# A hybrid decoder layer on Trainium2: the first 512 columns of x for the residual loaded behind the third branch block instead of behind the fourth

## The chip, the cores and the metric

The kernel runs on one core of one Trainium2 chip. The metric is the device time of one execution in microseconds (us). The core's engines are PE (TensorE, matrix products; PEld is its loading of weights), DVE (VectorE), ACT (ScalarE), POOL (GpSimd) and SP (SyncE, which issues most of the DMA transfers). Each engine works through its own instructions in order; they wait for each other and for DMA transfers through semaphores.

## What is computed

One layer of a decoder trunk over 256 tokens of width 2048, all in float32:

```
mod = silu(c) @ w_ada + b_ada;  shift1, scale1, gate1, shift2, scale2, gate2 = split(mod)
h = rms_norm(x, norm1_gain) * (1 + scale1) + shift1
proj = h @ w_in            # queries, keys, values of three branches, and 3 x 2048 columns of gates
y = sigmoid(g0) * (o_sb @ w_br_sb) + sigmoid(g1) * (o_dil @ w_br_dil) + sigmoid(g2) * (o_gla @ w_br_gla)
x = x + gate1 * (y @ w_out)
h = rms_norm(x, norm2_gain) * (1 + scale2) + shift2
x = x + gate2 * ((silu(h @ w_gate) * (h @ w_up)) @ w_ffn_out)
```

Here o_sb, o_dil and o_gla are the outputs of stick-breaking, dilated and gated linear attention. The change concerns the line `x = x + gate1 * (y @ w_out)`: where and when its x is loaded.

## The kernel before

**Products.** Every float32 product is made of three products of split operands: a value is the sum of a rounded high part and a remainder (`mm3`, L172 to L175). Weights come through `load_weights` (L140 to L170): SP loads 512 KB, two rows of 128 by 512 columns, into one of four `raw` buffers (L151), ACT casts it to `whi` (L165), DVE subtracts to `wlo` (L166). There are four buffers of each kind, so a load waits for the split of the load four before, and a cast waits for the matmuls that read the buffer four before. Such a double row is called a pair below: 12 matmuls of 512 columns in a block that works on both halves of the tokens (t = 0 and 1, 128 tokens each). `block` (L177) runs over k, 16 rows of 128 in y @ w_out, so eight pairs.

**Order of the work.** The program is traced by a framework that then orders the instructions of each engine itself: by priority among those that are ready. Priority is the place in the program; a stretch inside `prio()` is pulled forward by 4000 places. The loads, casts and splits of weights are pulled forward, and so are the residual (L1445) and the background loads of w_ada (L526, L527). The loads of x at L1439 are not.

**Named homes.** `S(tag, ...)` (L98) gives a buffer with a fixed home: a new tile under the same tag can be written once all readers of the old one have ended. Homes A2, A3, A4 and A8, 128 x 1024 float32 each, matter here. `gtags` (L1190) says which gates live there: A2, A3, A4 hold the three gates of the fourth block of 512 columns (and earlier those of the first); A8 holds the second branch's gate of the second block.

**Branch blocks.** `y_block(n)` (L1307) makes 512 columns of y: for each branch a product with its weights, then the gate times the product (L1318, L1320), then the sum (L1321). Gates of the first three blocks are made ahead; those of the fourth by `gate_block(3, br)` after the third branch block (L1343 to L1345). The last reader of A8's gate is therefore in y_block(1), those of the gates in A2, A3, A4 are in y_block(3).

**Output projection and residual.** After the branch blocks L1437 to L1440 load x in four parts of 512 columns, in the order of their use, into A2, A3, A4, A8 (`X2_TAGS`, L1404). Then L1441 to L1448 run three blocks of y @ w_out, 512 columns each, and a fourth follows at L1454 to L1467 with its tokens' halves one after the other. Each block accumulates in two PSUM buffers of a pool of four (`acc`, one for each t). `residual(n, t, ps)` (L1358) does, for each half of the tokens: a product of gate1 and the accumulator into a scratch tile (L1362, its only reader of the accumulator), an addition to x in place (L1363), and a sum of squares on ACT (L1365). The scratch tiles `scr` are three in turn. After both halves `put_away` (L1410) writes the new x to DRAM through the POOL queue; all four parts stay in their homes until the second norm has read them (L1374). Background work runs beside the blocks at given rates: loads of w_ada and their products on DVE (L431), with rates 0.85, 0.55 and 0.1 loads for each pair in the three blocks (`RATES_OP`, L35). Column sums of finished parts are turned on PE by four transposes at a time (L481).

Of the kernel before, what the change touches and what calls it, by code (L numbers as in the profile page):

```python
# [17 lines left out]
P = 128  # L18
T = 256
NT = T // P  # L20
# [3 lines left out]
NB = 512  # L24
# [56 lines left out]
def trunk(ctx: ExitStack, tc: tile.TileContext, I, out):  # L81
    nc = tc.nc
# [11 lines left out]
    def nm(base):  # L94
        uid[0] += 1
        return f"{base}_{uid[0]}"

    def S(tag, shape, dtype=F32):  # L98
        return slot.tile(shape, dtype, tag=tag, name=nm(tag))
# [13 lines left out]
    @contextmanager  # L113
    def prio(offset=AHEAD):

        with tc.high_priority(offset=offset):
            start = tc.cur_priority
            yield
            n = tc.cur_priority - start
        tc.cur_priority += n  # L120
# [56 lines left out]
    def block(pss, act, src, k0, k1, c0, base=0, w=None, tiles=range(NT), go_on=False, more=False, seeded=False,  # L177
              steps=None, pace=None):

        if w is None:
            w = load_weights(src, k0, k1, c0)
        if pace is None:
            pace = 1.0 if tiles[-1] == NT - 1 else 0.0
        for k in range(k0, k1):
            if (k - k0) % 2 == 0:
                tick(state["rate"] * pace)
            if k - k0 == DEFER and later:  # L190
                with tc.issue_after(state["mm"].ins), prio():
                    later.pop()()
            if steps and k - k0 in steps:
                with tc.issue_after(state["mm"].ins), prio():
                    steps[k - k0]()
            wh, wl = w[k - k0]
            for t in tiles:
                h, l = act(base + k, t)
                mm3(pss[t], h, l, wh, wl, k == k0 and not go_on, k == k1 - 1 and not more, seeded)
# [1052 lines left out]
    for j in range(2):  # L1252
# [3 lines left out]
        for t in range(NT):  # L1256
            for h in (2 * j, 2 * j + 1):
                o, c = og[t][:, h, :], t * N_GLA + h
# [5 lines left out]
    for j in range(2):  # L1264
        hi = S(gtag[0][j], [P, 4, T], F32R)
        lo = S(gtag[1][j], [P, 4, T], F32R)
        for t in range(NT):
            o = og[t].rearrange("p h d -> p (h d)")
            ps = misc_bank([P, 4, P])
            for i in range(4):  # L1270
                c = 4 * j + i
# [27 lines left out]
    def transpose_split(src, hi, lo, t, bank=misc_bank):  # L1299

        ps = bank([P, 4, P])
        for i in range(4):
            nc.tensor.transpose(ps[:, i, :], src[:, i * P : (i + 1) * P], ident)  # L1303
        c = slice(t * P, (t + 1) * P)
        split_from_psum(hi[:, :, c], lo[:, :, c], ps)

    def y_block(n, banks=(acc_bank, misc_bank, acc_bank)):  # L1307
        y = S("T3", [P, NT, NB])
        for br, (src, kc, act) in enumerate(
            ((I["w_br_sb"], 6, sb_at), (I["w_br_dil"], 2, dil_at), (I["w_br_gla"], 8, gla_at))  # L1310
        ):
            pss = [banks[br]([P, NB]) for _ in range(NT)]
            block(pss, act, src, 0, kc, n * NB)
            with prio():
                for t in range(NT):
                    g = gates[n, br][:, t, :]
                    if br == 0:
                        nc.vector.tensor_mul(y[:, t, :], g, pss[t])  # L1318
                    else:
                        nc.vector.tensor_mul(g, g, pss[t])  # L1320
                        nc.vector.tensor_add(y[:, t, :], y[:, t, :], g)  # L1321
        hi = S(ytags[n][0], [P, 4, T], F32R)
        lo = S(ytags[n][1], [P, 4, T], F32R)
        def turn():
            for t in range(NT):
                transpose_split(y[:, t, :], hi, lo, t)

        later.append(turn)
        yT.append((hi, lo))
# [9 lines left out]
    y_block(0, (misc_bank, acc_bank, acc_bank))  # L1339
    y_block(1)  # L1340
    y_block(2)
    state["rate"] = RATE_LAST
    for br in range(3):  # L1343
        gate_block(3, br)
# [8 lines left out]
    while "gate1" not in state:  # L1353
        tick(1)
    gate1 = state["gate1"]
    x2 = []
    x2ss = const.tile([P, NT, 4], F32, name="x2ss")
    def residual(n, t, ps):  # L1358

# [41 lines left out]
            nc.vector.tensor_tensor(h2[1][j][:, :, c], hf, hi.bitcast(F32), op=ALU.subtract)  # L1401

    h2_raw = {}
    X2_TAGS = ("A2", "A3", "A4", "A8")  # L1404
    x2_away = []

    def put_away(n):
# [10 lines left out]
    def gate2_bg():  # L1418

        acc = biased([S(tag, [P, 2 * NB]) for tag in ("OS0", "T3")], SEG_GATE2)  # L1420
        yield from ada_segment_steps(acc, SEG_GATE2, None, False, range(GATE2_CUT))
        yield from last_macs()
        for j in range(2):
            nc.gpsimd.dma_start(gate2_away[j], acc[j])
# [9 lines left out]

    ring["tags"] = ("A12", "KD", "KC", "H7")
    bg.append(gate2_bg())
    for n in range(4):  # L1437
        xr = S(X2_TAGS[n], [P, NT, NB])
        nc.sync.dma_start(xr, I["x"][:, n * NB : (n + 1) * NB].rearrange("(t p) c -> p t c", p=P))  # L1439
        x2.append(xr)  # L1440
    for n in range(3):  # L1441
        state["rate"] = RATES_OP[n]
        pss = [acc_bank() for _ in range(NT)]
# [192 lines left out]
    n, pss = 3, o[1]  # L1636
# [42 lines left out]
```

## Time and profile before

| what | value |
|---|---|
| three runs | 1582.02 us median (1581.56, 1582.02, 1584.25) |
| the profiled execution, its own time | 1581.39 us |
| its span, first to last instruction | 1579.6 us |
| mean granted clock of TensorE over the span | 0.999 |
| HBM read and written | 395.68 MB and 5.24 MB |
| DMA packets of the SP and ACT queues | 75.4% of 16 engines' span |

The times in the profile count from the start of the span. In a row of the timeline stand start, length, engine, line, operation, what is written and read, the count, and in brackets the idle time of that engine just before and what ended it. Buffer names are shown without their numbers, so A2 and A8 are both A. SPq is SP's queue of instructions: its rows are the issues of transfers. Rows of the view by stretches give the busy time of each engine in the stretch, the granted clock of TensorE (1.00 is full) and the share and rate of the DMA engines. In the list of waits stand who waited, for what, the total, the count and the longest. The ends of matmuls are modelled and overlap, so their pace is read from start to start.

### The profile page before, as it was taken

What the parts mean: (1) busy time and instruction counts of PE and PEld (TensorE: products, weight loads), DVE (VectorE), ACT (ScalarE), POOL (GpSimd) and SP (SyncE); (2) the same over time, 40 slices, a digit from 0 to 9 for tenths busy, and PEclk for the clock granted to TensorE, in tenths of its full rate; (3) what the DMA queues carried; (4) which work ended last, traced back from release to release, by engine and by line L of the source; (5) the groups of instructions that cost most, each with busy time, mean ns of one, the idle gap of its engine ahead of it and who ended that gap; (6) DMA issues with size and microseconds to landing.
All of it is one profiled execution on the core that took longest, in us unless ns stands there. A gap on an engine that the chain in (4) does not pass through costs nothing.

```text
span 1579.6 us, 20268 instructions
## 1 busy us (share of the span) xinstructions
PE 1564.1 (99%) x7177; PEld 1292.0 (82%) x7177; DVE 1407.4 (89%) x1728; ACT 879.7 (56%) x1222; POOL 12.6 (1%) x24
## 2 busy tenths in 40 slices
PE   8999999999999999999999999999999999999998
PEld 7878888888888888888877888888888888888887
DVE  6889996888899999987868889999999998989896
ACT  5654448875775554444435645566555555455553
POOL 1000000000000000000000000000000000000000
PEclk9999999999999999999999999999999999999999
DMA  9999987677797778988987897665656566876664
GB/s 336 360 326 323 335 302 240 222 224 223 242 310 255 235 246 267 304 300 309 334 301 252 286 320 228 198 200 200 198 192 222 174 200 236 283 228 201 225 209 138
DMA packets 196317, 402.26 MB, mean 255 GB/s; under 512 B 13102, under 2 KB 28116, under 8 KB 196216
## 3 DMA queue, kind: packets, MB, share of 16 engines
q1 hardware_dynamic: 194952, 397.75, 75.4%
q0 software_dynamic: 1088, 3.16, 0.5%
q8 instruction: 56, 0.92, 0.2%
q14 instruction: 45, 0.37, 0.1%
q10 hardware_dynamic: 176, 0.07, 0.0%
HBM read 395.68 MB, written 5.24 MB: 254 GB/s over the span
## 4 chain that ended last, share of the span: by engine, by line
PE 85%; DVE 6%; ACT 3%; DMA 3%; issue 2%; POOL 0%; SPq 0%; ACTq 0%; DVEq 0%; POOLq 0%
PE acc L175 20%; PE acc L174 20%; PE acc L173 20%; PE misc L173 7%; PE misc L175 7%; PE misc L174 7%; DVE wlo L229 1%; ACT whi L165 1%; DVE wlo L166 1%; DVE OD L229 1%; PE acc L586 1%; PE misc L955 1%; DVE KD L229 1%; DMA raw<-w_in 1%; PE misc L1303 0%
## 5 line engine op out<-in xcount | busy, mean ns | idle before, releaser
L165 ACT CAST whi<-raw 128x1024 fp32r<-128x1024 f32 (+1 forms) x277 | 279.1, 1012 | 287.4 <-PE acc L175 163.6
L166 DVE TENSOR_TENSOR wlo<-raw,whi 128x1024 fp32r<-128x1024 f32 (+1 forms) x277 | 321.9, 1172 | 88.5 <-ACT whi L165 86.9
L173 PE MATMUL acc<-whi,H 128*128 128x512 f32 x1006 | 394.2, 393 | 0.9 <-ACT H L598 0.8
L175 PE MATMUL acc<-whi,H 128*128 128x512 f32 x1006 | 392.7, 391 | 0.5 <-DVE H L605 0.4
L174 PE MATMUL acc<-wlo,H 128*128 128x512 f32 x1006 | 392.4, 390 | 0.8 <-DVE wlo L166 0.7
L175 PEld LDWEIGHTS acc<-whi,H 128*128 128x128 f32 x1006 | 188.7, 188 | 41.1 <-DVE H L605 1.6
L173 PEld LDWEIGHTS acc<-whi,H 128*128 128x128 f32 x1006 | 188.9, 188 | 39.6 <-ACT H L598 1.3
L174 PEld LDWEIGHTS acc<-wlo,H 128*128 128x128 f32 x1006 | 189.0, 188 | 39.3 <-DVE wlo L166 1.7
L243 ACT CAST whi<-raw 128x1024 fp32r<-128x1024 f32 (+1 forms) x130 | 125.5, 982 | 65.5 <-PE acc L175 28.0
L229 DVE TENSOR_TENSOR wlo<-raw,whi 128x1024 fp32r<-128x1024 f32 (+1 forms) x130 | 144.8, 1134 | 13.9 <-ACT whi L243 12.9
L173 PE MATMUL acc<-whi,A 128*128 128x512 f32 x211 | 83.2, 394 | 2.7 <-DVE scr L1362 2.7
L175 PE MATMUL acc<-whi,A 128*128 128x512 f32 x218 | 85.4, 392 | 0.0
L174 PE MATMUL acc<-wlo,A 128*128 128x512 f32 x211 | 82.7, 392 | 0.8 <-DVE wlo L166 0.8
L173 PE MATMUL misc<-whi,H 128*128 128x512 f32 (+1 forms) x209 | 81.0, 388 | 0.0
L175 PE MATMUL misc<-whi,H 128*128 128x512 f32 (+1 forms) x209 | 80.9, 387 | 0.0
L174 PE MATMUL misc<-wlo,H 128*128 128x512 f32 (+1 forms) x209 | 80.9, 387 | 0.0
L431 DVE SCALAR_TENSOR_TENSOR ada<-AR,csil,ada 128x1024 f32<-128x1024 f32 x38 | 48.2, 1280 | 6.0 <-DMA AR<-w_ada 6.0
L173 PEld LDWEIGHTS acc<-whi,A 128*128 128x128 f32 x211 | 39.9, 189 | 11.2 <-DVE scr L1362 3.1
L175 PEld LDWEIGHTS acc<-whi,A 128*128 128x128 f32 x218 | 41.2, 189 | 8.6
L243 ACT CAST whi<-OD 128x1024 fp32r<-128x1024 f32 (+1 forms) x25 | 25.5, 1020 | 40.7 <-DVE OD L229 21.8
L229 DVE TENSOR_TENSOR A<-raw,A 128x512 f32<-128x512 f32 (+2 forms) x53 | 47.2, 898 | 0.7 <-ACT A L243 0.2
L174 PEld LDWEIGHTS acc<-wlo,A 128*128 128x128 f32 x211 | 39.9, 189 | 9.3 <-DVE wlo L166 1.2
(714 smaller groups left out, 3035.6 us busy)
## 6 DMA issues: line engine op xcount, KB each, us to landing
raw<-w_in SPq DMA_DIRECT2D x189, 512.0 KB, 4.9
raw<-w_ffn_in SPq DMA_DIRECT2D x135, 512.0 KB, 4.6
raw<-w_ffn_out SPq DMA_DIRECT2D x73, 512.0 KB, 4.9
AR<-w_ada SPq DMA_DIRECT2D x59, 512.0 KB, 4.8
raw<-w_out SPq DMA_DIRECT2D x32, 512.0 KB, 6.6
OS<-w_ada SPq DMA_DIRECT2D x24, 512.0 KB, 6.9
AR<-w_ffn_in SPq DMA_DIRECT2D x22, 512.0 KB, 4.7
KC<-w_ada SPq DMA_DIRECT2D x21, 512.0 KB, 5.2
```

The costliest lines, as they stand in the source:

```text
L165: state["cast"] = nc.scalar.copy(hi[:, :n, :], raw[:, :n, :])
L166: state["split"] = nc.vector.tensor_tensor(lo[:, :n, :], raw[:, :n, :], hi[:, :n, :].bitcast(F32), op=ALU.subtract)
L173: nc.tensor.matmul(ps, lh, rh, start=start, stop=False, skip_group_check=seeded)
L174: nc.tensor.matmul(ps, lh, rl, start=False, stop=False, skip_group_check=seeded)
L175: state["mm"] = nc.tensor.matmul(ps, ll, rh, start=False, stop=stop, skip_group_check=seeded)
L229: done = nc.vector.tensor_tensor(dst, x, y, op=ALU.subtract)
L243: nc.scalar.copy(hi[:, :n, :], src)
L431: nc.vector.scalar_tensor_tensor(acc, raw, c, acc, op0=ALU.mult, op1=ALU.add)
L586: state["warm"] = nc.tensor.matmul(ps, ones_r, wide, start=True, stop=True)
L955: nc.tensor.matmul(ps[:n, t * N_GLA + h, :].rearrange("p (s l) -> p s l", l=L), at(f, h, t)[:, :n], odd(at(f, h, t)), start=True, stop=True,)
```

## The change

The load of the first 512 columns of x is moved in the program from behind y_block(3) to behind y_block(2), and the homes are dealt anew: the first columns go to A8, the second, third and fourth to A2, A3 and A4. The other three loads stay where they were. Nothing else is changed; no instruction is added or left out.

```diff
     y_block(2)
+    X2_TAGS = ("A8", "A2", "A3", "A4")
+    x2 = []
+
+    def load_x2(n):
+
+        xr = S(X2_TAGS[n], [P, NT, NB])
+        nc.sync.dma_start(xr, I["x"][:, n * NB : (n + 1) * NB].rearrange("(t p) c -> p t c", p=P))
+        x2.append(xr)
+
+    load_x2(0)
     state["rate"] = RATE_LAST
     for br in range(3):
         gate_block(3, br)
...
     gate1 = state["gate1"]
-    x2 = []
...
     h2_raw = {}
-    X2_TAGS = ("A2", "A3", "A4", "A8")
     x2_away = []
...
     bg.append(gate2_bg())
-    for n in range(4):
-        xr = S(X2_TAGS[n], [P, NT, NB])
-        nc.sync.dma_start(xr, I["x"][:, n * NB : (n + 1) * NB].rearrange("(t p) c -> p t c", p=P))
-        x2.append(xr)
+    for n in range(1, 4):
+        load_x2(n)
     for n in range(3):
         state["rate"] = RATES_OP[n]
```

## Prediction

> **What bounds the kernel now.** I read the page's shares first, then the waits of the stretch of the output projection (797 to 870 us), then the chain of waits there, then the instructions in order of time on SP, DVE and PE. The share line of the page:
>
> ```profile
> PE 1564.1 (99%) x7177; PEld 1292.0 (82%) x7177; DVE 1407.4 (89%) x1728; ACT 879.7 (56%) x1222; POOL 12.6 (1%) x24
> ```
>
> PE (TensorE) is busy for 1564.1 of the span's 1579.6 us. So nothing but PE time counts: a change gains what PE waits, or runs slowly, because of the thing changed, and no more. The load of x for the residual shows up in that way. The waits of the stretch 797 to 870 us (total, times, longest):
>
> ```profile
> DVE A L1363 <- DMA A<-x: 4.4, 1, 4.4
> ...
> PE acc L173 <- DVE scr L1362: 2.7, 1, 2.7
> ```
>
> One DVE addition waits for x, and PE waits once for a DVE product. The chain that ended last ties the two together (start, length, what):
>
> ```profile
> 820.73 6.67 DMA A<-x
> 827.42 0.69 DVE A L1363
> 828.11 0.61 DVE scr L1362
> ```
>
> The load of x issued at 820.73 lands 6.67 us later; the addition L1363 (first half of the tokens, columns 0 to 511) takes 0.69; behind it on the in-order DVE queue stands L1362 of the second half, which reads the accumulator that PE wants back. SP's queue says why the load is late, and what an empty A8 is worth:
>
> ```profile
> 654.97 0.37 SPq L1439 DMA_DIRECT2D A<-x  x1
> ...
> 820.31 0.37 SPq L151 DMA_DIRECT2D raw<-w_out  x1
> 820.73 0.46 SPq L1439 DMA_DIRECT2D A<-x  x1
> 823.03 0.37 SPq L151 DMA_DIRECT2D raw<-w_out  x1
> 823.45 0.98 SPq L1439 DMA_DIRECT2D A<-x  x2
> ```
>
> Four loads come from L1439. One is out at 655, three at 820 to 824. The names leave the number of A out, but the homes tell them apart: A2, A3 and A4 hold gates of the fourth block, and their last readers run after 760 us; A8 holds a gate of the second block. DVE's rows for the last reader of A8 (L1321) and of A2 (L1318):
>
> ```profile
> 653.66 1.29 DVE L1321 TENSOR_TENSOR T<-T,A 128x512 f32<-128x512 f32 x2
> ...
> 760.56 1.31 DVE L1318 TENSOR_TENSOR T<-A,acc 128x512 f32<-128x512 f32 x2
> ```
>
> So the load at 654.97, right as A8's last reader ends at 654.95, is that of the **last** 512 columns, which nobody needs before the fourth product block; the first 512 columns, needed first, wait behind weights until 820.73, though A2 is free from 761.87 (760.56 + 1.31).
>
> **What the wait costs PE.** PE in order of time, a normal passage first and then the wait:
>
> ```profile
> 802.49 0.39 PE L175 MATMUL acc<-whi,A 128*128 128x512 f32 x1
> 802.72 0.60 PE L481 MATMUL misc<-ident,ada 128*128 128x128 f32 x4
> 803.07 0.48 PE L173 MATMUL acc<-whi,A 128*128 128x512 f32 x1
> ```
>
> ```profile
> 825.71 0.39 PE L175 MATMUL acc<-whi,A 128*128 128x512 f32 x1
> 828.76 0.80 PE L173 MATMUL acc<-whi,A 128*128 128x512 f32 x1 [2.67 <-DVE scr L1362]
> 829.36 0.63 PE L174 MATMUL acc<-wlo,A 128*128 128x512 f32 x1
> 829.78 0.63 PE L175 MATMUL acc<-whi,A 128*128 128x512 f32 x1
> ...
> 831.49 0.87 PE L481 MATMUL misc<-ident,ada 128*128 128x128 f32 x4
> 832.12 0.48 PE L173 MATMUL acc<-whi,A 128*128 128x512 f32 x1
> ```
>
> Count from start to start. Normal: a matmul starts 0.23 us after the one before (802.49 to 802.72), and four transposes take 0.35 (802.72 to 803.07). From 825.71, undisturbed, PE would come to 825.94, after six matmuls to 827.32 and after the transposes to 827.67. It comes there at 832.12. The wait costs **832.12 - 827.67 = 4.45 us**, of which 2.82 are the late start (828.76 - 825.94) and 1.63 the slow six matmuls and transposes behind it. Those are slow because of the clock (stretch; busy time of PE, PEld, DVE, ACT, POOL; granted PE clock; DMA share; GB/s):
>
> ```profile
> 797.00:820.50 23.50, 23.50 (x111) 19.40 (x111) 17.03 (x17) 8.41 (x8) 0.00 (x0) 1.00 0.89 304
> 820.50:826.10 5.60, 5.59 (x25) 4.31 (x23) 1.23 (x1) 1.05 (x1) 0.00 (x0) 1.00 0.99 349
> 826.10:828.80 2.70, 0.04 (x1) 0.04 (x1) 1.35 (x3) 0.66 (x2) 0.00 (x0) 0.97 1.04 391
> 828.80:832.00 3.20, 3.20 (x9) 2.51 (x10) 1.93 (x3) 1.01 (x4) 0.57 (x1) 0.50 0.64 256
> ```
>
> The granted clock is 0.50 for the 3.20 us after the idle time. The Trainium skill (page TensorE: Matmul & The Clock Gate, Part 1) has the clock fall to half after an idle window of about 3.4 us; taken literally, 2.67 us would be too short, the sum would be 2.82 and the time 1579.2. The trace disagrees: the half clock stands right behind these 2.67 us, the measurement decides, and I give that case no chance of its own.
>
> **The change part by part.** *The load.* Its count stays four: one early, into A8, three late, into A2, A3, A4. x[0] takes the early place. A8 is free at the same moment and the new code stands earlier in program order, so I put the load at 655 us, 140 us before its reader. The SP queue at 655 gets the same 0.37 us entry as before. Gain: 4.45 us.
>
> *What moves with it.* The first residual can now follow its matmuls:
>
> ```profile
> 797.07 0.68 DVE L1362 TENSOR_TENSOR scr<-T,acc 128x512 f32<-128x512 f32 x1
> 797.67 2.36 DVE L166 TENSOR_TENSOR wlo<-raw,whi 128x1024 fp32r<-128x1024 f32 x2
> 801.39 1.23 DVE L166 TENSOR_TENSOR wlo<-raw,whi 128x1024 fp32r<-128x1024 f32 x1 [1.37 <-ACT whi L165]
> ```
>
> L1363, L1362, L1363, three instructions or 0.69 + 0.68 + 0.69 = 2.06 us, move from 827 to about 798. Cover: the splits at 797.67 are the third and fourth pair of the second w_out block, which begins near 797.6; the third is wanted two pairs of 12 x 0.23 us later, at 803.1, and would be done at 798.9 + 2.06 = 801.0; 2.1 us are to spare. DVE also idles 1.37 us before 801.39. Cost 0; without the cover at most 2.06. Two squares on ACT move as well; ACT is busy for 8.41 of 23.50 us there.
>
> *The write-back* of x[0] (L1410, POOL queue) moves from 829.73 to about 800, into the stretch with the DMA share 0.89 at 304 GB/s: 524288 bytes / 304 GB/s = 1.72 us of transfer. The Trainium skill (DMA: Bandwidth & Descriptors, Issuing engines are not separate DMA queues) speaks against the change here: transfers of all queues share the same 16 engines and interleave, so the POOL queue is no way around. Cover: the casts wait longest for PE to give buffers back, so weights stand ahead of PE:
>
> ```profile
> ACT whi L165 <- PE acc L175: 15.8, 11, 3.7
> ```
>
> That is 15.8 us over 11 casts in 797 to 870. Cost 0; without cover 1.72.
>
> *What is late next.* Columns 512 to 1023 now go to A2 and take the old place, 820.73, landing at 827.42. PE doesn't need their accumulators: the third block uses the first block's, free since 798. But DVE's queue holds the split of the third block's fifth pair. The third block starts 24 matmuls before the gap, at 825.94 - 24 x 0.23 = 820.42; pair five is due at 820.42 + 48 x 0.23 + 0.35 = 831.8. Should DVE stand at L1363 until 827.42, then L1363, L1362, L1363 and a split (2.06 + 1.23) end at 830.7; through ACT (square 0.63 + 0.19, cast 1.05, from the rows of those lines, split 1.23, after the first 0.69) at 831.2 (827.42 + 0.69 + 0.63 + 0.19 + 1.05 + 1.23):
>
> ```profile
> 828.14 0.63 ACT L1365 ACTIVATE scr<-A 128x512 f32<-128x512 f32 x1 [6.39 <-DVE A L1363]
> 828.68 0.19 ACT L1365 ACTIVATION_READ_ACCUMULATOR scr<-A 128x1 f32 x1
> ```
>
> In time by 0.6 us: cost 0. Where splits stand ahead of the addition there is no issue at all.
>
> *The next PE wait* follows in the fourth block:
>
> ```profile
> 851.25 0.39 PE L173 MATMUL acc<-whi,A 128*128 128x512 f32 x1
> 852.46 0.50 PE L174 MATMUL acc<-wlo,A 128*128 128x512 f32 x1 [0.81 <-DVE wlo L166]
> ```
>
> 1.21 - 0.23 = 0.98 us. Its loads queue behind the held-up ACT and DVE of 822 to 828; without the hold-up they start earlier and it may vanish (-0.98), or DVE and ACT catch up in another order and it doubles (+0.98, my guess at a bound). I take 0.
>
> Sum: **-4.45 us**, ends -5.43 and -4.45 + 2.06 + 1.72 + 0.98 = +0.31. The profiled execution took 1581.39 us, its span 1579.6; the median of the three runs is 1582.02, 0.63 above. 1582.02 - 4.45 gives **1577.6 us**; the profiled execution should show a span near 1575.2. About 0.2% (3.16 us) is what a measurement of this kernel can tell from no change.
>
> **The rivals.**
>
> 1. *The wait passes to the second 512 columns, in part.* x[1] is issued one place later, at 823.45 as the second of the late loads was, and lands 6.69 later at 830.14. That is 2.4 us after the 827.7 at which L1363 in front of pair five just suffices. PE idles about 2.4: 1577.6 + 2.4 = 1580.0, or 1581.6 with the half clock behind it. For: a DMA share of 0.99 at 820 to 826. Against: the rows of SP show x served between weights at just that point. 15%.
>
> 2. *Slower: x[1] starves.* In the run before, SP came to x only as PE was running out of work; with PE going on, weight loads keep coming, and they go first. Place: DVE at L1363 of the second columns, in front of pair five's split. Price: 1 us of PE per us of landing past 827.7, and 1.63 of half clock. It decides from 830.5 (2.8 + 1.63 eat the 4.45). If x[1] goes out one pair's time (12 x 0.23 = 2.76) behind the last x load of before (823.94, the second of the two issues that fill 0.98 us from 823.45), at 826.7, it lands at 833.4: 5.7 + 1.63 - 4.45 = +2.9, **1584.9**. For: A2 lay free for 59 us (761.87 to 820.73) with nothing issued into it. Against: the third block asks for fewer background loads (rate 0.1 against 0.85 and 0.55), so SP should come to x sooner. 12%.
>
> 3. *The gain is given back later.* PE arrives 4.45 earlier at stages where DVE is 89% busy over the span; if one such stage keeps its old time but for 2 us, 1580. Against: DVE loses its own 4.4 us wait too. 8%.
>
> 4. *The load isn't early*: the order of SP keeps it near 820 in spite of A8. 1582.0. Against: A8 took an x at 654.97. 3%.
>
> **How the numbers follow.** Forecast 62% (own range 1576.1 to 1578.8: the ends of the next PE wait, and the 0.5 by which the fastest run shown lies under the median). Rival 1 15%, rival 2 12%, rival 3 8%, rival 4 3%. Faster by over 0.2%, below 1578.9: the forecast and a third of rivals 1 and 3 with smaller delays, less a little: 0.67. Slower, above 1585.2: rival 2 and the tails of 1: 0.13. Same: the rest, 0.20. The range must reach over rivals 1, 3 and 4 and leaves out rival 2 and some tails: 1575.4 to 1583.0, the low end being 1577.6 - 0.98 less again about 1.2 for later PE waits, an estimate.
>
> **What would show it.** An x load near 655 read near 798; the first additions and squares gone from 827 to 830; no PE wait on L1362; granted clock 1.00 from 797 to 850; L1410's first issue near 800; the same 0.23 us pace throughout the third block. It would be wrong if DVE waits for x at another addition in front of splits that PE needs, if the granted clock drops at another place, or if the wait at 851 grows by more than 1 us.

## The result and the profile after

Twenty runs of each kernel:

| | before | changed |
|---|---|---|
| median | 1581.82 us | 1578.80 us |
| range | 1577.80 to 1586.98 | 1577.94 to 1582.06 |
| profiled execution, its time | 1581.39 us | 1578.55 us |
| its span | 1579.6 us | 1576.7 us |

The ratio is 0.9983 (95% interval 0.9976 to 0.9990). The change gains 3.0 us; 4.45 was forecast. The forecast started from a median of 1582.02 for the kernel before, 0.2 above the 1581.82 here.

In the changed kernel the same code stands in other lines: L1362 is L1371 (product), L1363 is L1372 (addition), L1365 is L1374 (square), L1410 is L1418 (write-back), L1439 is L1348 (load of x). Its share line:

```profile
PE 1562.4 (99%) x7177; PEld 1291.2 (82%) x7177; DVE 1407.6 (89%) x1728; ACT 881.1 (56%) x1222; POOL 12.7 (1%) x24
```

The issues of x on SP's queue (start, length):

```profile
654.66 0.37 SPq L1348 DMA_DIRECT2D A<-x  x1
...
822.00 0.46 SPq L1348 DMA_DIRECT2D A<-x  x1
823.72 0.37 SPq L151 DMA_DIRECT2D raw<-w_out  x1
824.13 0.56 SPq L1348 DMA_DIRECT2D A<-x  x1
826.43 0.37 SPq L151 DMA_DIRECT2D raw<-w_out  x1
826.85 0.46 SPq L1348 DMA_DIRECT2D A<-x  x1
```

Again one load goes out at 655 and three from 820 on, in the homes that the change deals. The first is now that of the first columns; the second columns start at 822.00. PE at the place where it had waited 2.67 us runs on at 0.23 us from start to start:

```profile
825.73 0.39 PE L173 MATMUL acc<-whi,A 128*128 128x512 f32 x1
825.96 0.39 PE L174 MATMUL acc<-wlo,A 128*128 128x512 f32 x1
826.18 0.39 PE L175 MATMUL acc<-whi,A 128*128 128x512 f32 x1
```

The stretches (busy time of PE, PEld, DVE, ACT, POOL; granted clock; DMA share; GB/s) show the full clock where 0.50 had stood, and the DMA share still above 1 there (a packet counts whole in the stretch in which it starts):

```profile
820.50:826.10 5.60, 5.60 (x28) 4.66 (x27) 4.44 (x5) 2.10 (x2) 0.00 (x0) 1.00 0.88 271
826.10:828.80 2.70, 2.70 (x14) 2.23 (x13) 0.30 (x1) 0.00 (x0) 0.00 (x0) 1.00 1.06 406
828.80:832.00 3.20, 3.20 (x16) 2.65 (x15) 2.15 (x6) 1.75 (x4) 0.08 (x1) 1.00 1.06 380
```

DVE still waits for x, now for the second columns; PE does not follow it:

```profile
825.18 1.23 DVE L166 TENSOR_TENSOR wlo<-raw,whi 128x1024 fp32r<-128x1024 f32 x1
829.52 0.69 DVE L1372 TENSOR_TENSOR A<-A,scr 128x512 f32<-128x512 f32 x1 [3.12 <-DMA A<-x]
```

**Where the 2.9 us of span come from.** Three starts of PE in each kernel delimit the third block and the first half of the tokens of the fourth (48 matmuls; at 0.227 us each 10.9 us if PE never waits). Before, then changed:

```profile
820.49 0.39 PE L173 MATMUL acc<-whi,A 128*128 128x512 f32 x1
...
847.17 0.39 PE L173 MATMUL acc<-whi,A 128*128 128x512 f32 x1
...
859.16 0.39 PE L173 MATMUL acc<-whi,A 128*128 128x512 f32 x1
```

```profile
821.18 0.39 PE L173 MATMUL acc<-whi,A 128*128 128x512 f32 x1
...
843.41 0.39 PE L173 MATMUL acc<-whi,A 128*128 128x512 f32 x1
...
855.64 0.39 PE L173 MATMUL acc<-whi,A 128*128 128x512 f32 x1
```

The third block took 26.68 us (847.17 - 820.49) and takes 22.23: **-4.45**, the forecast to the hundredth. The half block behind it took 11.99 and takes 12.23: +0.24. PE's one wait there was 0.81 us at 852.46, on the same split of a weight, and is now

```profile
848.89 0.50 PE L174 MATMUL acc<-wlo,A 128*128 128x512 f32 x1 [1.02 <-DVE wlo L166]
```

The third block begins 0.69 later, and what follows 859 loses 0.6 more (the end moved by -2.9, 859.16 by -3.52). Neither hangs on the change as far as the profiles show. PE works in the same order in both kernels up to 819 and from 835 on, and 0.66 of the 0.69 are there at 731 us already; the 0.6 come in at 1190 us, with a wait of 0.74 that e1 and e8 below, which have the same order of instructions, don't have. An example of such a wait: in the changed kernel's execution PE waits 1.50 us at 506.51 (two matmuls 1.89 from start to start), where before there were 0.51:

```profile
504.62 0.39 PE L173 MATMUL acc<-whi,H 128*128 128x512 f32 x1
506.51 0.47 PE L173 MATMUL misc<-X,H 128*128 128x512 f32 x1 [1.50 <-DVE A L1279]
```

Such waits, near 276, 505 and 1190 us, come and go by 0.8 to 1.5 us each between executions of one and the same order of instructions. The four profiled executions of the changed kernel's order (the result, e1, e8 and e12) have spans of 1575.2 to 1579.3 us.

### The profile page after: what moved, and what is told of

Same layout as the page of the kernel before. It is cut to its first block, busy times and chain, and to the rows that moved or that the text cites. A ratio compares the mean times of both kernels' runs of the same rounds, so it can differ in the third digit from the quotient of the medians.

```text
span 1576.7 us, 20265 instructions
## 1 busy us (share of the span) xinstructions
PE 1562.4 (99%) x7177; PEld 1291.2 (82%) x7177; DVE 1407.6 (89%) x1728; ACT 881.1 (56%) x1222; POOL 12.7 (1%) x24
## 4 chain that ended last, share of the span: by engine, by line
PE 87%; DVE 5%; ACT 3%; DMA 2%; issue 2%; POOL 0%; DVEq 0%; ACTq 0%; POOLq 0%
PE acc L175 20%; PE acc L174 20%; PE acc L173 20%; PE misc L173 7%; PE misc L175 7%; PE misc L174 7%; ACT whi L165 1%; DMA raw<-w_in 1%; PE acc L586 1%; DVE wlo L166 1%; PE misc L955 1%; DVE wlo L229 1%; PE misc L1303 0%; DVE A L229 0%; DVE OD L229 0%
```

## The experiments

The theory: what is gained in the third block is the late start and the half clock, 2.82 + 1.63 us, and it is fixed; the fourth product block, which takes weights twice as fast for each matmul (one half of the tokens at a time), gives some of it back. Rivals: it is the place in the program and not the home that counts (e1, e2); the half clock has nothing to do with the wait; the give-back is chance. In the table, the third block and the first half of the fourth are read from the profile of each kernel as above; "late" counts x loads issued at 820 us or later.

| kernel | late | third block, us | half block, us | median, us (runs) | ratio to before (95%) |
|---|---|---|---|---|---|
| before | 3 | 26.68 | 11.99 | 1581.82 (20) | |
| changed | 3 | 22.23 | 12.23 | 1578.80 (20) | 0.9983 (0.9976 to 0.9990) |
| e1 home alone | 3 | 22.23 | 15.65 | 1579.10 (11) | 0.9986 (0.9977 to 0.9995) |
| e2 place alone | 3 | 27.52 | 11.05 | 1580.43 (10) | 0.9993 (0.9983 to 1.0002) |
| e3 all four early | 0 | 22.24 | 11.55 | 1578.08 (8) | 0.9978 (0.9967 to 0.9988) |
| e4 all pulled forward | 0 | 22.23 | 11.53 | 1582.80 (11) | 0.9997 (0.9984 to 1.0010) |
| e5 wait filled | 3 | 24.58 | 11.75 | 1581.43 (10) | 0.9998 (0.9986 to 1.0010) |
| e6 two early | 2 | 22.23 | 14.70 | 1577.86 (9) | 0.9971 (0.9961 to 0.9980) |
| e7 first pulled forward | 2 | 22.23 | 15.21 | 1582.22 (12) | 1.0001 (0.9990 to 1.0012) |
| e8 changed | 3 | 22.23 | 12.31 | 1579.45 (12) | 0.9980 (0.9970 to 0.9989) |
| e9 second alone late | 1 | 22.23 | 11.88 | 1579.98 (11) | 0.9989 (0.9980 to 0.9998) |
| e10 all four early | 0 | 22.23 | 11.27 | 1577.70 (8) | 0.9975 (0.9965 to 0.9985) |
| e11 two early | 2 | 22.23 | 14.06 | 1578.37 (11) | 0.9976 (0.9967 to 0.9985) |
| e12 changed | 3 | 22.23 | 13.79 | 1580.37 (11) | 0.9993 (0.9983 to 1.0003) |

e1 to e4, e5 to e8 and e9 to e12 ran together; the kernel before had medians of 1582.46, 1582.22 and 1580.96 beside them.

### e1: the home alone

```
-    X2_TAGS = ("A2", "A3", "A4", "A8")
+    X2_TAGS = ("A8", "A2", "A3", "A4")
```

All four loads stay at their old place in the program.

> Only the homes are dealt anew (A8, A2, A3, A4); all four loads stay in their old place behind the fourth branch block. Theory (the home decides when the first columns of x land, because the queue takes a load as soon as its home is free and weights leave room): the first x load goes out near 655 us, no PE wait on the residual's product near 826, granted clock 1.00 from 797 to 850, time 3 to 4.5 us under the kernel before, ratio 0.997 to 0.998, the same as the changed kernel. Rival (the place in the program decides): first columns land as late as before, near 827, ratio 1.000 with the PE wait of 2.7 us and the half clock.

The ordering puts out the same order of instructions as for the changed kernel on every engine, SP's issues included, and the first load goes out at the same time:

```profile
654.41 0.37 SPq L1439 DMA_DIRECT2D A<-x  x1
```

So the home does it all: the move in the program adds nothing. In time e1 lies at 0.9986 of the kernel before; 0.997 to 0.998 was expected. The third block is 22.23 us. But the half block is 15.65, 3.7 more than before. PE's two waits there, with the clock of the stretches around them:

```profile
847.42 0.50 PE L173 MATMUL acc<-whi,A 128*128 128x512 f32 x1 [1.01 <-ACT whi L165]
849.48 0.50 PE L174 MATMUL acc<-wlo,A 128*128 128x512 f32 x1 [1.55 <-DVE wlo L166]
```

```profile
842.00:849.60 7.60, 5.04 (x22) 3.64 (x21) 4.71 (x6) 4.22 (x6) 0.00 (x0) 1.00 0.69 229
849.60:853.20 3.60, 3.60 (x11) 2.85 (x12) 3.60 (x5) 2.05 (x4) 0.53 (x1) 0.63 0.83 263
```

Here the fourth block gave back most of the gain in one execution: the waits first, and the half clock again behind them. Over 11 runs the kernel is still as the changed one is.

### e2: the place alone

```
+    X2_TAGS = ("A2", "A3", "A4", "A8")
+    load_x2(3)
...
+    for n in range(3):
+        load_x2(n)
```

> Only the place: the homes stay as before (A2, A3, A4, A8) and the load of the last 512 columns, into A8, is traced behind the third branch block. Theory (home): nothing changes, ratio 1.000 within 0.001, the first columns at about 821 us, PE waits 2.7 us on the residual's product, granted clock about 0.5 for 3.2 us behind it. Rival (place): some of the 3 us is gained, ratio 0.998 to 0.999.

The load is written behind the third branch block, but it is that of the last columns, in A8: the early place goes to them, as before. The wait stays, 0.7 us longer in this execution, and the half clock with it:

```profile
829.78 0.52 PE L173 MATMUL acc<-whi,A 128*128 128x512 f32 x1 [3.40 <-DVE scr L1371]
```

```profile
826.10:829.50 3.40, 0.28 (x2) 0.00 (x0) 1.07 (x2) 0.34 (x1) 0.00 (x0) 1.00 1.01 381
829.50:833.00 3.50, 3.22 (x11) 2.61 (x11) 2.21 (x4) 1.59 (x5) 0.57 (x1) 0.59 0.58 229
```

The rival of the place falls on the profile. On every engine, SP's issues included, the order of instructions is that of the kernel before: e2 is that kernel once more. Yet its median, 1580.43, lies 2.0 us under the 1582.46 beside it. So medians of ten to thirty runs of one order can lie that far apart, and the profiles, not the times, carry what is said of single us below. (A load of the *first* columns at the early place but into A2 was not run.)

### e3: all four loads early

```
-    X2_TAGS = ("A8", "A2", "A3", "A4")
+    X2_TAGS = ("A8", "X0", "X1", "X2")
...
-    load_x2(0)
+    for n in range(4):
+        load_x2(n)
...
-    for n in range(1, 4):
-        load_x2(n)
```

X0 to X2 are homes whose last readers end before the loads go out, at 677 to 692 us.

> All four x loads behind the third branch block, into A8 and the homes of the third block's three gates (X0, X1, X2). The DVE wait of 3.1 us for the second columns near 826 goes in either case. Theory: that wait cost PE nothing, and the PE wait of 1.4 us near 848 hangs on the end of the third block (cast, split, load, cast, split behind it), so the time equals that of the changed kernel within 0.5 us, ratio to before 0.998. Rival A: the hold-up of DVE and ACT delays the fourth block's weights and makes the wait near 848; then it shrinks and 1.0 to 1.2 us more are gained, ratio 0.9973 to 0.9976. Rival B: three more loads of 512 KB beside the gate block delay its weights; PE shows new waits between 665 and 760 and the gain shrinks by up to 5 us.

No DVE wait for x is left, PE has no wait in the half block, which takes 11.55 us, and none from 665 to 760. In the profile that is the expectation's rival A and not its theory. In the median the kernel lies 4.4 us under the kernel before (3.5 by the ratio) and 1.0 under e1; between e3 and e1 the times alone decide nothing (ratio of the medians 0.9994, 0.9982 to 1.0012). That 4.4 is near the forecast is chance: the forecast was for one early load.

### e4: all four loads pulled forward

The kernel before, with the load in `prio()`:

```
-        nc.sync.dma_start(xr, ...)
+        with prio():
+            nc.sync.dma_start(xr, ...)
```

> Homes and places as before, but the four loads are pulled forward in priority like the weights. Theory (what counts is that the first columns land before 797 us, in whatever home): they go into A2 as soon as it is free, near 762, land by about 772, no PE wait near 826, clock 1.00, time as the changed kernel, ratio 0.998. Rival: three loads of 512 KB (1.7 us of transfer each at 304 GB/s) ahead of the first weights of the output projection make PE wait there, up to 5 us near 770 to 785; ratio 0.999 to 1.001.

No gain: 1582.80. The last columns still go out into A8 at 656.53; the other three loads go out at 764.12, 768.73 and 778.92, two of them ahead of weights of the first product block, and ACT and then PE wait for those (the profiled execution, 1584.50 us, is the longest of the eleven):

```profile
778.10 1.04 ACT L165 CAST whi<-raw 128x1024 fp32r<-128x1024 f32 x1 [7.76 <-DMA raw<-w_out]
```

```profile
779.20 0.73 PE L173 MATMUL acc<-whi,A 128*128 128x512 f32 x2 [2.23 <-ACT whi L165]
```

```profile
779.00:783.00 4.00, 3.27 (x9) 2.32 (x10) 3.59 (x3) 3.10 (x4) 0.00 (x0) 0.72 1.07 388
```

The third block has its 22.23 us, but PE loses 4.9 us against the kernel before between 774 and 783. The rival came, the theory did not: an early load paid in these runs at 655 to 692 us, and not from 764 on.

### e5: the wait filled

Eleven matmuls whose result nobody reads are added to the kernel before: one ahead of the third block, ten in the wait.

```
...
+        if n == 2:
+            with tc.issue_after(state["k7"].ins), prio():
+                for _ in range(10):
+                    nc.tensor.matmul(idle, ones_r, yT[0][0][:, 0:2, :], start=True, stop=True)
```

> The kernel before with its late load of x kept, and with matmuls whose result nobody reads put into PE's wait: one ahead of the third block (0.23 us), ten (2.3 us) where PE waits for the residual's product near 826. Theory (the wait costs 2.8 us of late start and 1.6 us of half clock, and the half clock comes from the idle time): DVE's wait for x and the late start stay, but the granted clock stays 1.00 behind it; the third block's seventh matmul of the second token half comes 1.6 us earlier than before relative to the last matmul in front of the wait, 2.8 instead of 4.4 us late; time 1.4 to 1.6 us under the kernel before, ratio 0.999. Rival (the slow matmuls come from something else than idle time, DMA traffic at a share over 1.0 there or DVE's late splits): clock or pace stay slow, no gain, ratio 1.000.

PE's order of time in the wait, and the clock behind it:

```profile
826.60 2.49 PE L1457 MATMUL misc<-A,ones_r 128*128 128x512 f32 x10
828.93 0.39 PE L173 MATMUL acc<-whi,A 128*128 128x512 f32 x1
...
830.30 0.60 PE L485 MATMUL misc<-ident,ada 128*128 128x128 f32 x4
830.65 0.48 PE L173 MATMUL acc<-whi,A 128*128 128x512 f32 x1
```

```profile
828.80:832.00 3.20, 3.20 (x18) 2.64 (x17) 2.58 (x5) 2.05 (x6) 0.57 (x2) 1.00 0.79 305
```

The six matmuls and four transposes behind the wait now take 1.72 us (830.65 - 828.93); before they took 3.36 (832.12 - 828.76). The difference, 1.64, is the size of the prediction's half-clock term, 1.63, parted from the late start. That it was the filling that kept the clock up is not shown by this one execution, the fastest of its ten: 27 of 92 runs of the kernel before have a mean clock of 1.000 without any filling, and 5 of the 10 runs here are under it. The median of all runs, 0.8 under the kernel before beside it where 1.4 to 1.6 was expected (ratio 0.9998), can't show it either.

### e6: two early, two late

As e3, but with homes A8, X0, A3, A4 and only the first two loads early.

> The changed kernel, with the second 512 columns loaded early as well (into X0, free after the third block's first gate); the third and fourth still go out near 822 to 826 us. Theory after the last runs (the late second columns hold DVE 3 to 4.5 us and ACT 5 to 6 us, SP's loads for the fourth block come 5 us later, and PE pays 1.2 to 3 us near 846 for it): no DVE wait near 826, fourth-block loads at about 828, 831, 833 and 836, PE's wait near 846 under 0.5 us, time as with all four early, 0.8 to 1.2 us under the changed kernel. Rival (it is the traffic of the three late loads, DMA share 1.06 there, that delays the weights): two of three stay, so most of the PE wait near 846 stays, 0 to 0.4 us under the changed kernel.

DVE no longer waits for the second columns. The median, 1577.86, is the lowest of the four that ran together, 1.6 us under the changed kernel (e8). But the theory's sign, a PE wait near 846 of under 0.5 us, isn't there. The profiled execution, at 1581.36 us the longest of the nine, took 14.70 us for the half block, 2.7 more than before:

```profile
849.74 0.79 PE L174 MATMUL acc<-wlo,A 128*128 128x512 f32 x1 [1.55 <-DVE wlo L166]
```

```profile
850.00:853.40 3.40, 3.40 (x9) 2.68 (x10) 3.40 (x5) 2.77 (x6) 0.53 (x1) 0.54 0.83 246
```

### e7: the first load alone pulled forward

The kernel before, with the load of the first columns in `prio()`, home A2.

> Homes and places as before; only the load of the first 512 columns is pulled forward like the weights, into A2. Theory (three loads ahead of the first weights of the output projection cost PE 4.9 us near 776, late start and half clock together; the weights stand about one load behind there): with one load, 1.7 us of transfer, PE's wait near 776 is under 1.2 us and the clock stays 1.00; the wait near 826 is gone; the time is 0.5 us slower to 0.5 us faster than the changed kernel, ratio 0.998 to 0.9985. Rival (any load pulled ahead of those weights pushes them past a limit): PE waits over 2 us near 776 with the half clock, ratio 0.9995 to 1.000.

The load goes out at 760.93, and the third block is 22.23 us again, so A2 serves that block as well as A8. The median is that of the kernel before. That is the rival's time without its reason: near 776 PE waits only 0.53 us, at full clock, as the theory had it. In the profile the loss is in the fourth block, where PE waits 0.56 and 1.55 us and the clock halves:

```profile
PE acc L174 <- DVE wlo L166: 2.1, 2, 1.6
PE acc L173 <- ACT whi L165: 0.6, 1, 0.6
```

```profile
850.00:853.40 3.40, 3.40 (x10) 2.64 (x9) 3.40 (x5) 1.99 (x4) 0.53 (x1) 0.54 0.77 240
```

### e8: the changed kernel again

> The changed kernel again, for comparison on the same chip: 2.5 to 3.5 us under the kernel before, ratio 0.998 to 0.9986; DVE waits 3 to 4.5 us for the second columns near 826 with no PE wait there; PE waits 1.2 to 3 us near 846.

1579.45 us and 0.9980: here the result repeats; in e12 it doesn't to this size. The half block is 12.31 us, PE's wait in it 1.14 us at 847.76.

### e9 to e12: what costs the half block its weights

Two ways were open. *Hold-up*: DVE stands at the addition of the second columns, and the splits queue behind it. *Traffic*: the late loads of x push weight loads back. e9 has the hold-up with one late load; e6 and e11 have two late loads without the hold-up; e10 has neither.

```
-    X2_TAGS = ("A8", "A2", "A3", "A4")
+    X2_TAGS = ("A8", "A2", "X1", "X2")
...
-    load_x2(0)
+    for n in (0, 2, 3):
+        load_x2(n)
...
-    for n in range(1, 4):
-        load_x2(n)
+    load_x2(1)
```

> Homes A8, A2 and two gate homes that are empty by the third branch block; parts one, three and four of x are loaded behind the third branch block, the second alone late, into A2. It parts the two ways in which the late loads can cost the fourth product block its weights. Theory (hold-up): DVE stands at the addition of the second columns until that load lands, and the splits queue behind it. DVE should then still wait 2 to 4 us for x near 826 to 829, the fourth block's first half of the tokens should take 12 us or more (10.9 is its length without a wait), and the time should be that of the changed kernel, near 1579. Rival (traffic): the 1.5 MB of three x loads at 822 to 827 push the weight loads back. With 0.5 MB in their place, the first half should take 11 to 11.6 us as with all four loads early, in spite of DVE's wait, and the time should lie near 1578.

> The same program as e3_early_all, all four loads early. The first run gave 1578.08 us and a ratio of 0.9978 to the kernel before; if the give-back at the fourth block is what the changed kernel lacks, it should again lie 0.5 to 1.5 us under the changed kernel in this same call, and most of its runs should show a mean granted clock of 1.000. If the first result was chance, the two agree within 0.3 us.

> The same program as e6_early_two, the first two parts early, the last two late. If the hold-up of DVE is what costs the fourth block its weights, its first half should take under 12 us in this profile and the 14.7 of the first profile was one run's own; if the traffic of the late loads does it, it should be above 12 again. Time near 1578, as before (1577.86, ratio 0.9971).

> The changed kernel once more, on the same chip as the three versions above, as the measure for them: 1579 us, ratio to the kernel before 0.998, stage of the third block 22.2 us, first half of the fourth block's tokens 12 to 12.5 us. If early loads help beyond the change, it lies 0.5 to 1.5 us above e10 and e11.

In e9 DVE waits for the second columns (in e9 to e11 the lines stand one further down), and PE idles for 0.63 us in the half block, 11.88 us long:

```profile
830.58 0.69 DVE L1373 TENSOR_TENSOR A<-A,scr 128x512 f32<-128x512 f32 x1 [3.15 <-DMA A<-x]
```

```profile
849.53 0.50 PE L174 MATMUL acc<-wlo,A 128*128 128x512 f32 x1 [0.63 <-DVE wlo L166]
```

In e11 DVE doesn't wait for x, but 4.16 us for a weight at 837.78, because ACT waits for the transfer. PE waits twice in the half block; the clock stays full there:

```profile
836.70 1.05 ACT L165 CAST whi<-raw 128x1024 fp32r<-128x1024 f32 x1 [4.33 <-DMA raw<-w_out]
837.78 1.22 DVE L166 TENSOR_TENSOR wlo<-raw,whi 128x1024 fp32r<-128x1024 f32 x1 [4.16 <-ACT whi L165]
```

```profile
849.50 0.51 PE L173 MATMUL acc<-whi,A 128*128 128x512 f32 x1 [1.06 <-ACT whi L165]
851.56 0.50 PE L174 MATMUL acc<-wlo,A 128*128 128x512 f32 x1 [1.55 <-DVE wlo L166]
```

```profile
849.60:853.20 3.60, 2.05 (x8) 1.47 (x9) 3.60 (x6) 2.61 (x4) 0.00 (x0) 1.00 0.62 191
```

In e10 PE's list of waits for 797 to 870 has one entry left:

```profile
PE misc L1395 <- DVE ada L1383: 0.2, 1, 0.2
```

In e12, the changed kernel, PE waits as in e11, and the clock stays full too. With a half block of 13.79 us (12 to 12.5 expected), 1580.37 us and a ratio of 0.9993 (0.998 expected) whose interval reaches over 1, e12 missed its expectation:

```profile
849.07 0.50 PE L173 MATMUL acc<-whi,A 128*128 128x512 f32 x1 [0.75 <-ACT whi L165]
851.12 0.50 PE L174 MATMUL acc<-wlo,A 128*128 128x512 f32 x1 [1.55 <-DVE wlo L166]
```

By the length of the half block the **profiles** speak for traffic: without late loads it takes 11.27 to 11.55 us, with one 11.88, with two or three 12.2 to 15.7, whether DVE waits for x or not (among the kernels whose third block takes 22.2 us; in the others PE comes to the half block 2 to 5 us later, with more of its weights there). So the give-back is no chance of one execution: all seven profiles with two or three late loads, the changed order's four among them, lie over all three without. The rows in between show both ways at work. Hold-up: SP issues no weight load between 826.43 and 833.20 in the changed kernel and none between 827.45 and 834.25 in e9, while e10 has three (828.50, 829.93, 832.52). Traffic: of the weight loads issued from 822 to 833.5 us, those whose landing the profile shows took 5.4 to 6.2 us in e10, 6.3 to 7.9 in e6 and 8.0 to 9.3 in e11. The **times** don't decide. e9 isn't under the changed kernel beside it (ratio of the medians 0.9998, 0.9984 to 1.0006), while e11 is (0.9987, 0.9976 to 0.9994; these intervals come from drawing the runs anew), which would speak for the hold-up; but drawn in the same way e2 lies at 0.9987 (0.9979 to 0.9996) of the kernel before, whose order of instructions it has. The profiled executions of e6 and e11, 1581.36 and 1581.66 us, are the longest of their kernels' runs, so their half blocks may not be the usual ones. Which of the two ways weighs more stays open. With all four loads early neither is left: PE has no wait in the half block in e3 and e10. In time e10 lies 2.7 us under the changed kernel beside it (0.9983, 0.9970 to 0.9990), 0.5 to 1.5 expected, and e3 1.0 under e1.

Against the kernel before, all four early stands at 0.9978 and 0.9975 of its time, two early at 0.9971 and 0.9976. That either is faster than the changed kernel is likely and not shown by these runs; which of the two is better is open.

**How often the clock falls.** Each run lists its mean granted clock over the span, and one window at half clock, 3.41 us long in the trace of the kernel before (0.50 from 828.63 to 832.04), makes it 0.999 (half of 3.41 in 1580 is 0.001). The mean doesn't say where the window stood. In the three groups of four kernels, 65 of 92 runs of the kernel before show less than 1.000; of the changed kernel 3 of 20 beside the result and 15 of 34 in e1, e8 and e12; of two early 8 of 20, of all four early 2 of 16. Among runs at 1.000 alone the median of the changed kernel still lies under that of the kernel before beside it, by 2.2 us (e1), 3.3 (e8) and 0.4 (e12), from 6 or 7 such runs of the changed kernel each: the gain doesn't come from the clock alone, but these runs don't settle its size without it.

## Why the prediction was right in direction and too large

- **What bounds the kernel; the wait as a PE loss of 4.45 us.** Right: in every kernel whose first x was early the third block fell from 26.68 to 22.23 or 22.24 us. e5 separates the size of its half-clock part (1.64 measured, 1.63 forecast). The product of this step, 4.45 us in this block, is right; it isn't what the whole kernel gains.
- **The home is what makes the load early.** Right: the load went out at 654.66, and e1 shows that the home alone does it; in e2 the early place with the old homes changes nothing.
- **Residual and write-back moved at no cost.** Right. The products and additions came between splits, at 797.75 to 803.15, and PE's pace stayed 0.23 us; the first write-back went out at 804.13 instead of near 800.
- **The second columns take the late place, cost 0.** Right for the third block, but not by the margin that was worked out: issued at 822.00 and read at 829.52, they came 2.1 us later than forecast, past the 827.7 from which rival 1 let PE wait (828.0 by the prediction's own margin of 0.6 us). PE paid nothing because the other case held that the prediction named, splits ahead of the addition (the last at 825.18). Rivals 1 and 2, a wait there, didn't come in any profile.
- **The next PE wait, taken as 0.** This step failed. The half block took 12.23 us in the changed kernel's first profile, 12.31 in e8, 13.79 in e12 and 15.65 in e1, against 11.99 before: 0.24 to 3.66 us, where the bound was 0.98. Rival 3, a gain given back later, came in part, and not where DVE is busiest but where weights are short. In the first profile PE comes to the half block 3.76 us earlier (843.41 instead of 847.17), the cast that waits longest there for its weight starts 3.56 us earlier (844.79 instead of 848.35). The price that was left out is the clock: behind a wait of 1.55 us there the half clock stood in e1, e6 and e7 (about 1.7 us, half of 3.41) and not in e11 and e12.
- **One profile as the price.** This term was mis-sized. The half clock was taken as certain, because it was in the profiled execution; over the runs 65 of 92 show such a window, somewhere. So at most 1.63 x 65 / 92 = 1.15 us of the 1.63 was to be had on average, an estimate. That accounts for 0.5 of the 1.4 us that the measured gain lacks; how the rest is shared between the fourth block and windows elsewhere is not shown. The time without the half clock, 1579.2, which the prediction set aside, lies nearer to the measured 1578.80 than its 1577.6: the half clock did follow the wait in that execution, but not in every one.

The forecast's likelier case, a gain of over 0.2%, stayed just out of reach: by the ratio the gain is 0.17%. With twenty runs of each kernel an interval of 0.07% to each side still parts it from nothing; with the eleven of e12 it doesn't.

Of the signs that were named, the load, the missing PE wait, the pace and the clock of 1.00 from 797 to 850 are there. "DVE waits for x at another addition" is there as well, 3.12 us, and PE paid nothing for it at once. The two other signs of being wrong, a drop of the clock at another place and a wait at 851 that grows by more than 1 us, are not in the first profile (0.81 and 1.02 us, clock 1.00), but e1, the same order of instructions, has both (two waits, 2.56 us together), and e12 the second (2.30 together).

**The clock rule.** The prediction set the row, half clock behind 2.67 us of idle time, above the figure of the Trainium skill. The runs go further: in e6 a single wait of 1.55 us had the half clock behind it, in e1 waits of 1.01 and 1.55, while waits of 1.06 and 1.55 in e11 and of 0.75 and 1.55 in e12 had none, nor had one of 2.17 us in e3 (clock 1.00 from 508 to 518):

```profile
508.01 0.47 PE L173 MATMUL misc<-X,H 128*128 128x512 f32 x1 [2.17 <-DVE A L1279]
```

In the fourteen profiles the clock fell seven times while PE was at work, each time from 0.13 us before the end of such a wait (the kernel before) to 1.20 us after it (e11, at 34.26, behind waits of 0.48 and 0.80). That fits idle time as the cause of the half clock; the length of the wait alone doesn't decide. The Trainium skill (TensorE: Matmul & The Clock Gate, Part 1) says that the window which the clock looks at runs freely and doesn't start with the program, so that the point of change varies from run to run. That agrees with waits of one length that do and don't bring the drop; its length of about 3.4 us of idle time doesn't agree with 1.55.

## What to carry to other kernels

When several transfers share a set of homes, first ask which of them gets the home that comes free early, and give it to the one that is needed first; the place of the load in the program did nothing here, the home did everything (a higher priority made it early too, in e4 and e7, and the gain was lost elsewhere). A wait taken from one block brings the tensor engine earlier to the next: price the next block's supply of weights by its own pace, and count as a cost the half clock that a new wait of 1.5 us there can bring. Take a term that hangs on the clock times how often it comes; the mean granted clock of many runs gives an upper bound for that.

## What was not expected of the hardware

- A half-clock window of about 3.4 us followed waits of 1.55 us (clock 0.54 at 850.00 to 853.40 in e6) and of 1.01 and 1.55 (0.63 at 849.60 to 853.20 in e1), and didn't follow 1.06 and 1.55 in e11 (1.00 at 849.60 to 853.20).
- One order of instructions (the changed kernel and e1) had half blocks of 12.23, 12.31, 13.79 and 15.65 us in four profiled executions: the same loads served by the same queues differ by 3.4 us at one place.
- Three loads of x issued at 764 to 779 us, beside the first weights of the output projection, cost PE 4.9 us there, as much as the early x gained at 826 (e4); at 677 to 692 three cost nothing that the runs show (e3, e10).
